# Moving second-product copies and squares from VectorE to ScalarE in the first groups of an MLP, and shifting a list of conditioning sums by a step

## The chip, the cores and the metric

The kernel runs on one core of one Trainium2 chip. The metric is the device time of one execution in microseconds (us); lower is better. The engines carry the profile's names: PE is TensorE's matmuls and PEld its weight loads, DVE is VectorE, ACT is ScalarE, POOL is GpSimd, and SP is SyncE, which issues the DMAs.

## The reference, cut to what matters

The program is a two-layer diffusion backbone over 512 latent tokens and 256 context tokens of width 1024. Each layer is a token mixer (pooling in layer 0, attention in layer 1) and then an MLP with 4096 inner units:

```python
def sq_relu_mlp(h, w_in, w_out):
    return jnp.square(jax.nn.relu(h @ w_in)) @ w_out
...
        m_lat = sq_relu_mlp(modulate(rms_norm(x, g_mlp_pre[i]), sh2, sc2), w_mlp_in[i], w_mlp_out[i])
        x = x + gt2 * rms_norm(m_lat, g_mlp_post[i])
```

The shift, scale and gate vectors come from the conditioning vectors `c` (latent tokens) and `c_ctx` (context tokens):

```python
def ada_mods(cond, w, b):
    m = (jax.nn.silu(cond) @ w + b)[..., None, :]
    return jnp.split(m, N_MOD, axis=-1)
```

All values are fp32.

## The kernel before

**Arithmetic.** A matrix product in fp32 accuracy is made of three products of rounded operands: each operand is split into a high part (a copy in the rounded type, usually on ACT) and a low part (operand minus high part, on DVE), and PE adds high x high, high x low and low x high.

**The first MLP (`mlp0`).** The 768 tokens are six row tiles of 128. The 4096 inner units are 16 groups of 256. For each group there is a first product (tokens by `w_mlp_in`), then ReLU and square, then a second product (squares by `w_mlp_out`), which is added up over the groups in the array `acc`. Group 0 and group 1 make the first product in the ordinary way (class `Inner`, line 553 for the matmuls). Later groups use a scheme with seven block products instead of eight (class `Seven`, line 672); it needs sums of blocks of the tokens, made once in `sums` (lines 617 to 620), and sums of blocks of the weights, made for each group in `weights_sums` (lines 638 to 655).

**Squares.** `Inner.square` takes the ReLU of a half group (`r`), squares it on ACT straight into the high part (line 572), squares it again on DVE into a tile `q` (line 573), and subtracts (line 574). `Seven.run` does it in another way: it squares in place on ACT (698), copies to the high part on ACT (699) and subtracts on DVE (700).

**The second product.** `out_mm` makes it for one row tile: two banks of 512 columns and twelve matmuls (line 768). There are four such banks in all (pool `psB`), which other small products share. `out_ev` takes the banks to `acc`. For group 0 it copies (line 776), for later groups it adds (line 780). Two of the six tiles, 1 and 4, are "seeded" in later groups: ACT copies the running sum from `acc` into the banks first (line 760), PE adds onto it, and ACT copies the result back (line 778). The seeding of a tile is left out while a counter `stale` is above zero; `ada_fin` sets it to 4, and each `out_mm` lowers it by 2. The weights of the second product are split into one slot (lines 126 and 129), which is free again when the matmuls of the group before are done.

**Conditioning sums.** A part of the shift, scale and gate vectors is computed beside the MLP on DVE: `ada_sum` loads 1 MB of `w_ada` and multiplies it by the conditioning vector, one instruction for each of eight blocks and each condition (lines 263 and 268), then transposes and reduces (271, 272). A list `work` holds 24 such sums, alternating between one for two conditions and one for a single condition. `ada_step` takes the next from the list. It is called at the start of a group (`extra0`, from group 1 on) and in the middle of `Seven.run` (`mid0`, groups 1 to 13), 27 times in all. Three calls after the fourth sum of a vector, `ada_fin` closes the vector: eight small matmuls (line 280) and an addition. Loads go through three staging buffers (`raw`), shared by the weights of the MLP and `w_ada`.

**Spilled rows.** Before the MLP the residual rows `xr` (six tiles) are written to memory (`spill_rows`, line 594), since `sums` reuses their place; `before0` closes that place again and loads the rows back ahead of the last stage, `finish`. The tiles' rows are made in the order 4, 5, 0, 1, 2, 3.

**Order.** The compiler plans the order on each engine: each engine executes its own instructions strictly in that order and waits where an operand or a place isn't ready. Instructions given to `keep_in_program_order` keep their place; in the first stage this holds for the loads that SP issues.

Of the kernel before, what the change touches and what calls it, by code (L numbers as in the profile page):

```python
# [12 lines left out]
AF = mybir.ActivationFunctionType  # L13
ALU = mybir.AluOpType
# [8 lines left out]
TOK = LAT + CTX  # L23
NL = LAT // P
NT = TOK // P
# [28 lines left out]
def backbone(ctx: ExitStack, tc, x, c, ctx_in, c_ctx, w_ada, b_ada, g_mix_pre, g_mix_post,  # L54
# [3 lines left out]
    sy, ve, sc, gp, te = nc.sync, nc.vector, nc.scalar, nc.gpsimd, nc.tensor  # L58
# [9 lines left out]
    def residents(stack):  # L68
        pool = stack.enter_context(tc.tile_pool(name="residents", bufs=1, side="right"))
        return (pool.tile([P, NT, D], F32, name="xr"), pool.tile([P, 2, D], F32, name="gate"),  # L70
                pool.tile([P, D], BF16, name="junk"))
# [40 lines left out]
    def work_tile():  # L112
        return tmp.tile([P, D], F32, tag="t", name="work")

    def sm_tile(tag):
        return small.tile([P, 8], F32, tag=tag, name=tag, bufs=2 if tag == "gc" else 8)
# [124 lines left out]
    def ada_out(i, m, j, ps, nc_, w=2):  # L241
        at = m * KT + 2 * j
        ve.tensor_tensor(out=mods[i][:, at:at + w, 0:nc_], in0=ps.rearrange("p (b c) -> p b c", c=nc_),
                         in1=cols[:, i * 48 + at: i * 48 + at + w].unsqueeze(2).broadcast_to([P, w, nc_]),
                         op=ALU.add)
        if (i, m) == (0, SH1):
            ve.tensor_scalar(out=minus[:, 2 * j:2 * j + w], in0=mods[i][:, at:at + w, 0:nc_], scalar1=-1.0,
                             scalar2=None, op0=ALU.mult)
        if m in (SC1, SC2):
            s = 0 if m == SC1 else 1  # L250
            g0 = 96 + s * 16 + i * KT + 2 * j
            ve.scalar_tensor_tensor(out=avec[i][s][:, 2 * j:2 * j + w, 0:nc_], in0=mods[i][:, at:at + w, 0:nc_],
                                    scalar=1.0,
                                    in1=cols[:, g0:g0 + w].unsqueeze(2).broadcast_to([P, w, nc_]),
                                    op0=ALU.add, op1=ALU.mult)
# [19 lines left out]
    def ada_fin(i, m, parts, nc_):  # L275
        n = 4 * nc_
        ps = psB.tile([P, 512], F32, tag="b", name="psada")
        stale[0] = 4
        for a in range(4):
            te.matmul(ps[32 * a:32 * a + 32, 0:2 * n], sel,  # L280
                      parts.rearrange("p (u c b a) -> p a u b c", c=nc_, b=2, a=4)[:, a], start=True, stop=True)
        ada_out(i, m, 0, ps[:, 0:2 * n], nc_, 8)
# [23 lines left out]
    def gate_diag(i, m, ci, to=None):  # L306
        to = ci if to is None else to
        gc = gate_cols(i, m, ci)
        gh = small.tile([P, 2, KT], F32R, tag="gh", name="gh", bufs=2)
        ve.tensor_copy(gh[:, 0, :], gc)  # L310
        ve.tensor_tensor(out=gh[:, 1, :], in0=gc, in1=gh[:, 0, :], op=ALU.subtract)
        dg = [tmp.tile([P, KT, P], F32R, tag="t", name="diag") for _ in range(2)]
        for z, d in enumerate(dg):
            ve.tensor_tensor(out=d, in0=ident.unsqueeze(1).broadcast_to([P, KT, P]),
                             in1=gh[:, z, :].unsqueeze(2).broadcast_to([P, KT, P]), op=ALU.mult)
        for h in range(2):
            ps = psB.tile([P, 512], F32, tag="b", name="psg")
            for z, d in enumerate(dg):
                te.matmul(ps, onesr[:, 0:1].broadcast_to([P, P]), d[:, 4 * h:4 * h + 4, :], start=(z == 0), stop=(z == 1))
            sc.copy(gate[:, to, 512 * h:512 * h + 512], ps)  # L320
# [210 lines left out]
    class Inner:  # L531
# [36 lines left out]
        def square(self, f):  # L568
            hi, lo = self.hid
            r = self.relu(f)  # L570
            q = work_tile()[:, 0:self.ntok]
            sc.activation(hi[:, f, :], r, AF.Square)
            ve.tensor_tensor(out=q, in0=r, in1=r, op=ALU.mult)
            ve.tensor_tensor(out=lo[:, f, :], in0=q, in1=hi[:, f, :], op=ALU.subtract)
# [15 lines left out]
    S = {}  # L590

    def spill_rows():
        for t in (4, 5, 0, 1, 2, 3):
            tc.keep_in_program_order(sy.dma_start(spill[:, t], xr[:, t]))

    def sums():
# [175 lines left out]
    def out_ev(i, parts, t, cols=HALVES):  # L772
        for (c0, w), ps in zip(cols, pso[t]):
            d = accv[:, t, c0:c0 + w]
            if parts[0][0] == 0:
                ve.tensor_copy(d, ps)
            elif seeded[t]:
                sc.copy(d, ps)
            else:
                ve.tensor_tensor(out=d, in0=d, in1=ps[:, 0:w], op=ALU.add)  # L780

    def finish(i, parts, order, last, also=()):
        st = Steps()
        for z in also:
            st.at(*z)
        for n, t in enumerate(order):
            cols = THIRDS if (i, t) == (1, NL - 1) else HALVES
            st.at(5.2 * n, out_mm, i, parts, t, cols)
            st.at(5.2 * n + 5.2, out_ev, i, parts, t, cols)
            last(st, n, t)  # L790
        st.run()

    def mlp0(inner, hids, order, extra, mid, last, before_last):
        aH, aL = inner.a
        one = lambda z: Ring([z], True)
        wi = w_in(0, 1, one(unit[1]), True)
        spill_rows()
        for f in range(2):
            inner.square(f)
        wo_ = w_out(0, 0, one(unit[2]))  # L800
        sums()
        for g in range(NG - 1):
            if g:
                wo_, products = w_out(0, g, one(unit[2])), weights_sums(g + 1)
            part = (g, inner.hid, wo_)
            extra(g)
            if g:
                inner = Seven(products, hids[(g + 1) % len(hids)])
            else:
                inner = Inner(g + 1, wi, aH, aL, hids[(g + 1) % len(hids)], chunks0, TOK)  # L810
            inner.run((lambda: mid(g)) if g < NG - 2 else None)
            if g == NG - 2:
                wo_ = w_out(0, NG - 1, one(unit[1]))
            else:
                for t in range(NT):
                    out_mm(0, [part], t)
                    out_ev(0, [part], t)
        before_last()
        finish(0, [part, (NG - 1, inner.hid, wo_)], order, last)
# [128 lines left out]
    work, due = [], []  # L948
# [4 lines left out]
    def ada_step():  # L953
        for u in [u for u in due if u[0] <= 0]:
            ada_fin(*u[1:])
        due[:] = [(u[0] - 1, *u[1:]) for u in due if u[0] > 0]
        if work:
            i, m, nc_, j, at = work.pop(0)
            ada_sum(i, m, j, nc_, parts[0][:, at + 8 * nc_ * j:at + 8 * nc_ * j + 8 * nc_])
            if j == 3:  # L960
                due.append((2, i, m, parts[0][:, at:at + 32 * nc_], nc_))
# [5 lines left out]
    def head_gains():  # L967
        sy.dma_start(grow[:, 0, :], g_q[0].partition_broadcast(P))
        sy.dma_start(grow[:, 1, :], g_k[0].partition_broadcast(P))
        ve.tensor_scalar(out=grow[:, 0, :], in0=grow[:, 0, :], scalar1=float(HD) ** -0.5, scalar2=None, op0=ALU.mult)  # L970

    def extra0(g):
        if g == 1:
            pinned[0] = False
        if g == 4:
            head_gains()
        if g:
            ada_step()
        if g == 2:
            sc.activation(sm_tile("sm")[:, 7:8], nhalf[:, 0:1], AF.Exp)  # L980
# [68 lines left out]
    def w_chunk(ch, kk, wait=None, pin=False):  # L1049
        chunks.setdefault(ch, []).append(  # L1050
            qring[0].load(w_qkv[0, 512 * kk:512 * kk + 512, 512 * ch:512 * ch + 512]
                      .rearrange("(k p) n -> p k n", p=P), 512, pin, wait))
# [90 lines left out]
    def before0():  # L1143
        nonlocal xr, gate, junk
        S["held"].close()
        xr, gate, junk = residents(held[1])
        gate_diag(0, GT2, 0)
        gate_diag(0, GT2, 1)
        for t in (4, 5, 0, 1, 2, 3):
            sy.dma_start(xr[:, t], spill[:, t])  # L1150
        qring.append(Ring([unit[0], unit[2], unit[1]]))
        w_chunk(2, 0, raw0)
# [169 lines left out]
    def last1(st, n, t):  # L1322
# [3 lines left out]
        st.at(5.2 * n + 7.8, fin_b, t)  # L1326

    mlp0(first[0], hids0, (4, 5, 0, 1, 2, 3), extra0, mid0, last0, before0)
    mlp1(first1[0], last1)

# [53 lines left out]
```

## Time and profile before

| | us |
|---|---|
| median of 3 runs | 1190.38 (1189.02 to 1190.64) |
| the profiled execution's own time | 1189.55 |
| its span, first to last instruction | 1187.8 |
| PE busy in the span | 1147.0 |
| DVE busy | 950.5 |
| ACT busy | 624.1 |

The profile is one execution. A span is the time from its first to its last instruction; the execution's own time is 1.75 us longer. "Busy" is the time in which an engine had an instruction in work, and an engine may be busy and still not be what sets the end. A row of the order of time gives start, duration, engine, line, operation, output and inputs; in brackets stand the idle time ahead of it and the instruction that ended it. "Granted clock" is the share of its full clock at which PE was let run.

### The profile page before, as it was taken

The numbers are of one execution on the slowest core, as the hardware profiler recorded it, in microseconds if no ns is written. First come the engines' busy times: TensorE is split into PE (matmuls) and PEld (weight loads), VectorE is DVE, ScalarE is ACT, GpSimd is POOL, SyncE is SP. The second block draws the span as 40 slices with busy tenths as digits, with TensorE's granted clock in tenths as the row PEclk, the third lists the DMA queues.
The fourth block names the chain that finished last, engine by engine and source line by source line (L and its number), as shares of the span: only waits on it lengthen the run. The fifth ranks groups of instructions, "written<-read, shape, count | busy, mean of one in ns | idle before, by whom it ended". The sixth has DMA issues, their size and how long they took to land.

```text
span 1187.8 us, 15989 instructions
## 1 busy us (share of the span) xinstructions
PE 1147.0 (97%) x6170; PEld 990.3 (83%) x6170; DVE 950.5 (80%) x1564; ACT 624.1 (53%) x1063; POOL 67.7 (6%) x120
## 2 busy tenths in 40 slices
PE   5899999999999999999999999999899999999997
PEld 3679789989899889988887889998888888888886
DVE  3787968889889888986587689978687788778876
ACT  4666435443445444544576378872676346435522
POOL 2030000000000000000142210001100000000001
PEclk9899999999999999999999999999999999999999
DMA  9984134443444443333431301105344133314312
GB/s 338 363 292 178 36 107 142 142 142 107 144 136 146 142 142 95 130 131 107 179 105 36 107 1 36 37 4 195 122 141 154 46 120 133 113 39 142 107 33 109
DMA packets 100011, 147.84 MB, mean 124 GB/s; under 512 B 2736, under 2 KB 75872, under 8 KB 99936
## 3 DMA queue, kind: packets, MB, share of 16 engines
q1 hardware_dynamic: 99936, 146.84, 36.6%
q8 instruction: 48, 0.79, 0.3%
q14 instruction: 27, 0.22, 0.1%
HBM read 139.49 MB, written 7.34 MB: 124 GB/s over the span
## 4 chain that ended last, share of the span: by engine, by line
PE 47%; issue 33%; DVE 9%; ACT 5%; POOL 3%; DMA 2%; SPq 0%; POOLq 0%; DVEq 0%; ACTq 0%
PE pso L768 19%; PE psin L672 17%; PE po L1226 2%; PE psq L1015 2%; PE pss L1187 2%; POOL rs L169 1%; DVE rows L268 1%; PE psin L553 1%; DMA raw<-in_w_mlp_in 1%; POOL rs L1024 1%; ACT junk L154 1%; DVE sm L1191 1%; PE psada L225 1%; PE pspt L1212 1%; DVE units L129 1%
## 5 line engine op out<-in xcount | busy, mean ns | idle before, releaser
L768 PE MATMUL pso<-units,rb 128*128 128x512 f32 x1152 | 279.7, 394 | 4.0 <-ACT pso L760 2.9
L768 PEld LDWEIGHTS pso<-units,rb 128*128 128x128 f32 x1152 | 215.7, 189 | 47.9 <-ACT pso L760 3.6
L268 DVE SCALAR_TENSOR_TENSOR rows<-raw,cond,rows 128x256 f32<-128x256 f32 x280 | 122.0, 477 | 0.7
L780 DVE TENSOR_TENSOR acc<-acc,pso 128x512 f32<-128x512 f32 x135 | 88.5, 676 | 31.6 <-PE pso L768 31.3
L553 PE MATMUL psin<-ra,rb 128*128 128x512 f32 (+1 forms) x432 | 104.8, 342 | 2.4 <-ACT ra L363 1.6
L872 PE MATMUL pso<-units,pairs 128*128 128x512 f32 x336 | 82.3, 389 | 0.0
L553 PEld LDWEIGHTS psin<-ra,rb 128*128 128x128 f32 x432 | 70.3, 189 | 13.6 <-ACT ra L363 1.9
L553 PE MATMUL psin<-ra 128*128 128x512 f32 x256 | 80.6, 389 | 0.0
L872 PEld LDWEIGHTS pso<-units,pairs 128*128 128x128 f32 x336 | 63.1, 188 | 13.1
L876 DVE TENSOR_TENSOR acc<-acc,pso 128x512 f32<-128x512 f32 x72 | 48.6, 681 | 27.6 <-PE pso L872 27.6
L167 POOL TENSOR_SCALAR ms<-ss 128x1 f32<-128x1 f32 x20 | 11.4, 572 | 1010.5 <-ACT junk L154 998.8
L672 PE MATMUL psin<-ra,units 128*128 128x384 f32 x336 | 66.0, 338 | 0.7 <-ACT psin L684 0.6
L672 PE MATMUL psin<-sums,units 128*128 128x384 f32 x336 | 63.7, 337 | 0.3 <-ACT units L638 0.2
L672 PEld LDWEIGHTS psin<-ra,units 128*128 128x128 f32 x336 | 59.3, 188 | 4.2 <-ACT psin L684 0.9
L129 DVE TENSOR_TENSOR units<-raw,units 128x1024 fp32r<-128x1024 f32 (+2 forms) x49 | 55.2, 1151 | 7.3 <-ACT units L126 7.1
L672 PEld LDWEIGHTS psin<-sums,units 128*128 128x128 f32 x336 | 58.8, 188 | 2.4 <-ACT psin L680 0.7
L760 ACT COPY pso<-acc 128x512 f32<-128x512 f32 x42 | 24.3, 589 | 67.2 <-DVE acc L780 65.2
L553 PEld LDWEIGHTS psin<-ra 128*128 128x128 f32 x256 | 48.0, 188 | 10.0
L126 ACT CAST units<-raw 128x1024 fp32r<-128x1024 f32 (+2 forms) x49 | 47.2, 995 | 14.3 <-PE pso L768 10.3
L553 PE MATMUL psin<-rb 128*128 128x512 f32 (+1 forms) x144 | 52.7, 367 | 0.2 <-DVE rb L364 0.2
L1015 PE MATMUL psq<-units,ra 128*128 128x512 f32 x216 | 51.7, 392 | 0.0
L553 PE MATMUL psin<-rb,ra 128*128 128x512 f32 x128 | 49.8, 389 | 0.0
(253 smaller groups left out, 2350.2 us busy)
## 6 DMA issues: line engine op xcount, KB each, us to landing
raw<-in_w_ada SPq DMA_DIRECT2D x48, 1024.0 KB, 5.4
raw<-in_w_mlp_in SPq DMA_DIRECT2D x32, 1024.0 KB, 5.4
raw<-in_w_mlp_out SPq DMA_DIRECT2D x32, 1024.0 KB, 5.1
raw<-in_w_qkv SPq DMA_DIRECT2D x6, 1024.0 KB, 5.3
spill<-xr SPq DMA_DIRECT2D x10, 512.0 KB, 9.3
xr<-spill SPq DMA_DIRECT2D x10, 512.0 KB, 5.9
raw<-in_w_o SPq DMA_DIRECT2D x4, 1024.0 KB, 5.4
xr<-in_x SPq DMA_DIRECT2D x4, 512.0 KB, 4.4
```

Of the source, the lines that this page charges most:

```text
L126: a = sc.copy(hi, raw)
L129: b = ve.tensor_tensor(out=lo, in0=raw, in1=hi, op=ALU.subtract)
L268: ve.scalar_tensor_tensor(out=r, in0=raw[:, k, :], scalar=cond[:, k, c:c + 1], in1=r, op0=ALU.mult, op1=ALU.add)
L553: te.matmul(ps[:, bank, o:o + ln], w[:, k, fs], rhs, start=start, stop=(k == KT - 1 and n == 2), skip_group_check=len(ks) < KT)
L672: te.matmul(bank, w[k], a[k], start=start and k == 0 and m == 0, stop=stop and k == 3 and m == 2, skip_group_check=True)
L760: sc.copy(ps, accv[:, t, c0:c0 + w])
L768: te.matmul(pss[h][:, 0:cols[h][1]], a[:, f, ts_], w[:, f, cols[h][0]:sum(cols[h])], start=(n == 0 and not seeded[t]), stop=(n == len(seq) ...
L780: ve.tensor_tensor(out=d, in0=d, in1=ps[:, 0:w], op=ALU.add)
L872: te.matmul(ps, a, w, start=(m == 0), stop=(m == len(seq) - 1))
L876: ve.tensor_tensor(out=M[n][:, t], in0=M[n][:, t], in1=ps, op=ALU.add)
L1015: te.matmul(ps, a[:, k, sl], w[:, k % 4, :], start=(k == 0 and n == 0), stop=(k == KT - 1 and n == 2))
L1187: te.matmul(ps[:, c2, 0:384], a[:, sl], b[:, kv, 384 * c2:384 * c2 + 384], start=(n == 0), stop=(n == 2))
```

## The change

It has five parts, all around the first MLP. (1) `Inner.square` for 768 tokens, which is groups 0 and 1, works as `Seven.run` does: it squares in place on ACT, copies to the high part on ACT, subtracts on DVE, and no tile `q` is needed. (2) In group 0's second product, 8 of the 12 copies from the banks to `acc` go from DVE to ACT; DVE keeps the right halves of tiles 1, 2, 4 and 5. (3) `extra0` no longer calls `ada_step` in group 1, so there are 26 calls, and every sum of the list is done one call later than before. (4) The last vector to be closed, whose time would be after the last call, is closed in `before0`. (5) The rows are spilled in the order 0 to 5.

```diff
         def square(self, f):
             hi, lo = self.hid
             r = self.relu(f)
+            if self.ntok == TOK:
+                sc.activation(r, r, AF.Square)
+                sc.copy(hi[:, f, :], r)
+                ve.tensor_tensor(out=lo[:, f, :], in0=r, in1=hi[:, f, :], op=ALU.subtract)
+                return
             q = work_tile()[:, 0:self.ntok]
...
     def spill_rows():
-        for t in (4, 5, 0, 1, 2, 3):
+        for t in range(NT):
             tc.keep_in_program_order(sy.dma_start(spill[:, t], xr[:, t]))
...
             if parts[0][0] == 0:
-                ve.tensor_copy(d, ps)
+                (ve.tensor_copy if c0 and t % 3 else sc.copy)(d, ps)
...
         if g == 4:
             head_gains()
-        if g:
+        if g > 1:
             ada_step()
...
     def before0():
         nonlocal xr, gate, junk
         S["held"].close()
+        assert not work
+        for u in due:
+            ada_fin(*u[1:])
         xr, gate, junk = residents(held[1])
```

## The prediction

> **What bounds the kernel now.** I read the page's busy shares first, then the table of stretches stage by stage, then PE in order of time where a stretch shows idle PE, and then who was late there. Part 1 of the page:
>
> ```profile
> PE 1147.0 (97%) x6170; PEld 990.3 (83%) x6170; DVE 950.5 (80%) x1564; ACT 624.1 (53%) x1063; POOL 67.7 (6%) x120
> ```
>
> PE sets the end, so a change can win only where PE idles or runs slower. This one works on the first MLP. Its stretches (length; busy time of PE, PEld, DVE, ACT, POOL with counts; granted clock; share and GB/s of DMA):
>
> ```profile
> 105.00:157.00 52.00, 48.37 (x245) 42.63 (x244) 50.85 (x80) 24.33 (x32) 0.00 (x0) 0.97 0.20 65
> 188.20:500.00 311.80, 310.71 (x1571) 277.67 (x1570) 279.06 (x529) 147.42 (x220) 0.00 (x0) 1.00 0.41 134
> ```
>
> The second row is the steady loop, ten groups of 31 us: PE is full but for 311.80 - 310.71 = 1.09 us, and DVE works some 28 us a group. The first row, in which the first groups start up, is the other way round: DVE is busy 50.85 of 52 us, PE lacks 3.63, ACT works less than half the time, and the clock is under 1. PE there, in order of time:
>
> ```profile
> 133.85 11.08 PE L768 MATMUL pso<-units,rb 128*128 128x512 f32 x48
> 145.38 0.73 PE L768 MATMUL pso<-units,rb 128*128 128x512 f32 x2 [0.46 <-ACT units L126]
> 148.09 0.50 PE L768 MATMUL pso<-units,rb 128*128 128x512 f32 x1 [1.97 <-ACT pso L760]
> 149.48 5.12 PE L768 MATMUL pso<-units,rb 128*128 128x512 f32 x13 [0.89 <-ACT pso L760]
> ```
>
> And the stretch right behind:
>
> ```profile
> 150.00:154.00 4.00, 4.00 (x11) 3.13 (x12) 4.00 (x6) 1.95 (x2) 0.00 (x0) 0.57 0.25 77
> ```
>
> Group 0's second product ends at 144.9 us; then PE waits 0.46 + 1.97 + 0.89 = 3.32 us. Behind that the clock falls: 4.00 us at 0.57 are 4.00 x 0.43 = 1.72 us of lost PE work. Together 5.04 us. Who caused the two longer waits:
>
> ```profile
> 147.45 0.59 ACT L760 COPY pso<-acc 128x512 f32<-128x512 f32 x1 [1.17 <-DVE acc L776]
> 148.12 0.68 DVE L776 COPY acc<-pso 128x512 f32<-128x512 f32 x1
> 148.84 0.59 ACT L760 COPY pso<-acc 128x512 f32<-128x512 f32 x1 [0.80 <-DVE acc L776]
> ```
>
> There are four banks for these products and a row tile takes two. Group 1's seeded tile needs the two of group 0's last tile, which PE had filled by 144.9, but whose copies stood in DVE's queue; the last began at 148.12, 3.2 us late. The chain of waits over 105 to 160 us names DVE lines for most of what isn't PE's own work:
>
> ```profile
> by line: PE pso L768 12.7%; DVE work L617 12.3%; DVE acc L776 12.3%; DMA raw<-in_w_mlp_in 9.2%; DVE rows L268 8.3%; issue 7.4%; PE psin L672 6.7%; DVE sums L620 6.4%; DVE units L129 6.4%; DVE rb L620 3.4%; DVE rb L574 3.3%; DVE work L573 3.
> ```
>
> **The change part by part.** Prices come from the groups of 105 to 157 us (count | busy us, mean ns | idle before):
>
> ```profile
> L776 DVE COPY acc<-pso 128x512 f32<-128x512 f32 x12 | 7.9, 681 | 0.0
> L268 DVE SCALAR_TENSOR_TENSOR rows<-raw,cond,rows 128x256 f32<-128x256 f32 x14 | 6.2, 475 | 0.0
> L573 DVE TENSOR_TENSOR work<-work 128x768 f32<-128x768 f32 x4 | 3.8, 952 | 1.0 <-ACT work L560 1.0
> L572 ACT ACTIVATE rb<-work 128x768 fp32r<-128x768 f32 x4 | 3.4, 848 | 0.1
> L619 ACT CAST sums<-work 128x768 fp32r<-128x768 f32 x6 | 5.0, 832 | 3.5 <-DVE work L617 2.0 <-DMA raw<-in_w_mlp_in 1.4
> L271 DVE STREAM_TRANSPOSE raw<-rows 128x256 f32<-128x256 f32 x2 | 0.8, 416 | 0.0
> L272 DVE TENSOR_REDUCE parts<-raw 128x16 f32<-128x512 f32 x1 | 0.7, 672 | 0.0
> L263 DVE TENSOR_SCALAR rows<-raw,cond 128x256 f32<-128x256 f32 x2 | 0.6, 349 | 0.0
> ```
>
> ACT makes the same copy out of these banks elsewhere (min/median/max ns):
>
> ```profile
> L778 ACT COPY acc<-pso x42: 564/588/593, 157.0 to 558.0; 128x512 f32<-128x512 f32 x42
> ```
>
> *Copies.* DVE keeps the right halves of tiles 1, 2, 4 and 5. Eight move: DVE -8 x 0.681 = 5.4 us, ACT +8 x 0.588 = 4.7 us. The last tile's two halves are then copied on two engines side by side.
>
> *Squares.* Four times, DVE loses L573 (3.8 us in all); ACT squares in place, as long as L572, and adds a copy like L619: 4 x 0.832 = 3.3 us. The high part comes some 0.84 us later. What hides that is the distance to its reader:
>
> ```profile
> 109.40 0.85 ACT L572 ACTIVATE rb<-work 128x768 fp32r<-128x768 f32 x1
> 126.26 5.64 PE L768 MATMUL pso<-units,rb 128*128 128x512 f32 x24
> 145.26 0.95 DVE L574 TENSOR_TENSOR rb<-work,rb 128x768 fp32r<-128x768 f32 x1
> ```
>
> Group 0's squares of 109.4 are first multiplied at 126.3. Group 1's low part ended at 146.2, out of DVE's backlog, and comes earlier without it.
>
> *First conditioning sum.* 6.2 + 0.8 + 0.7 + 0.6 = 8.3 us leave DVE in this stretch. They are moved, not saved: the list still has 24 sums, and the last one falls into group 13's start instead of group 12's middle.
>
> Sum for the stretch: DVE 50.85 - 5.4 - 3.8 - 8.3 = 33.4 of 52, ACT 24.33 + 4.7 + 3.3 = 32.3. Neither is the bound then; PE is. DVE's lateness of 3.2 us stands against 17.5 us taken off its queue, so I count the two longer waits as gone.
>
> What is late next is the split of group 1's output weights, since its slot is free only when PE is through with group 0's:
>
> ```profile
> 144.29 1.99 ACT L126 CAST units<-raw 128x1024 fp32r<-128x1024 f32 x2 [5.60 <-PE pso L768]
> ```
>
> With ACT's half copy (1.0 us) and DVE's subtraction (1.2 us, half of the 2.35 in the steady loop's row below) the first low half is there at 146.5. If PE has nothing else from 145.4 on, it waits 1.1 us; if group 2's products are ready, because the weight sums come earlier, it waits 0. Ends 0 and 1.1; I take 0.5, since ACT, now with 32 us, may hold one copy back. Whether such a rest would still pull the clock down, these rows tell:
>
> ```profile
> 851.11 1.53 PE L349 MATMUL psx<-ident,acc 128*128 128x128 f32 x12 [1.60 <-DVE acc L514]
> 854.28 0.50 PE L553 MATMUL psin<-ra,rb 128*128 128x256 f32 x2 [1.64 <-ACT ra L363]
> ```
>
> ```profile
> 800.00:900.00 100.00, 96.54 (x508) 82.87 (x508) 75.06 (x106) 55.74 (x87) 8.74 (x17) 1.00 0.46 154
> ```
>
> Waits of 1.60 and 1.64 us close together left the clock at 1.00, so 1.1 us should too. The Trainium skill ("TensorE: Matmul & The Clock Gate", section Why this matters for your kernels) asks only that PE-idle gaps stay under about 3 us. By that rule alone three gaps of at most 1.97 us would not explain the fall at 150 us, its 1.72 us need not go with them, and the gain would be 1.72 us less. The trace bears this out at 851 us and speaks against it at 145 us.
>
> *The list moved by a step.* Sums for two conditions and for one alternate. So far the former ran at a group's start and the latter in its middle; now it is the reverse, and the middle is where DVE is dense:
>
> ```profile
> 203.11 0.48 DVE L268 SCALAR_TENSOR_TENSOR rows<-raw,cond,rows 128x256 f32<-128x256 f32 x1
> 213.90 2.35 DVE L129 TENSOR_TENSOR units<-raw,units 128x1024 fp32r<-128x1024 f32 x2
> 217.79 5.19 PE L768 MATMUL pso<-units,rb 128*128 128x512 f32 x22
> 222.82 2.27 PE L672 MATMUL psin<-ra,units 128*128 128x384 f32 x12
> ```
>
> Beginning with the one at 203.11, five single L268 stand ahead of the weight split at 213.90. Doubled, each adds 0.4 us or so (back to back nine take 3.64, next fence), and the opening multiply 0.26: 2.3 us. The first half of the split ends near 215.1 and is needed at 217.79: slack 2.7 us. It holds by 0.4 us, and PE could bring the product of 222.82 forward (2.27 us). I take 0. The ends are one irregular group, which is there already:
>
> ```profile
> 412.43 3.64 DVE L268 SCALAR_TENSOR_TENSOR rows<-raw,cond,rows 128x256 f32<-128x256 f32 x9
> 432.78 0.73 PE L768 MATMUL pso<-units,rb 128*128 128x512 f32 x2 [0.68 <-ACT units L126]
> 433.73 0.62 PE L672 MATMUL psin<-sums,units 128*128 128x384 f32 x2 [0.21 <-ACT units L638]
> ```
>
> It paid 0.68 + 0.21 = 0.89 us after sums had run as a block. Ends: -0.9 if it becomes regular, +10.7 if all twelve groups become like it.
>
> *Closing steps.* Each finished vector closes half a group later, the last one just ahead of the last stage; instructions are the same. Two groups instead of five lose the seed of tile 1, so six adds on DVE become six seeds and six copies on ACT; in the steady loop ACT has 147 of 312 us. 0, with cover on both engines.
>
> *Spill order.* SP issues the same six transfers, but tiles 4 and 5 behind tile 3, whose rows are written last; the output weights queued behind them start about two issues, 0.8 us, later.
>
> ```profile
> DMA to landing us min/median/max: 8.7/10.0/12.1
> 86.14 1.62 SPq L107 DMA_DIRECT2D raw<-in_w_mlp_out  x2
> 113.26 0.84 ACT L619 CAST sums<-work 128x768 fp32r<-128x768 f32 x1 [1.38 <-DMA raw<-in_w_mlp_in]
> ```
>
> Issued by 87, the spills land by 99; what overwrites the rows starts at 113.26. 0. The dropped sum's load isn't dropped: the next sum's block takes its place and holds its staging buffer longer, which leaves two for weights; the steady loop lives with that.
>
> Sum against the profiled execution's 1189.55 us: -3.32 - 1.72 + 0.5 = -4.5, so 1185.0. The median of the runs, 1190.38, lies 0.83 above that execution: 1185.9.
>
> **The rivals.**
>
> *Slower: the reversed sums hold up every group.* If the two-condition sum runs ahead of the weight split as a block, each of twelve groups pays 0.89 us: 1185.9 + 10.7 = 1196.6. It ends slower by over 0.2% from (4.5 + 2.4) / 12 = 0.58 us a group. For it: DVE's 28 of 31 us and a slack of only 0.4. Against: PE lost 1.09 us in ten groups in all.
>
> *No change: the stall stays in another form.* If group 1's product again stands directly behind group 0's in PE's fixed order and the longest gap and the slow clock stay, 0.46 + 0.89 = 1.35 us go: 1189.0. For it: the order is planned beforehand, not chosen by readiness. Against: the late engine loses a third of its work.
>
> *ACT becomes the bound.* If in each of six tiles one copy holds PE for its 0.588 us, 3.5 us come back: 1189.4. For it: eight of twelve copies in one queue with squares and splits. Against: 32 of 52 us.
>
> **How the numbers follow.** Forecast 0.62, stall stays 0.15, ACT 0.08, sums 0.15. About 0.2%, 2.4 us, is what a measurement of this kernel tells from no change. Of the sums' 0.15, 0.03 cost so little that it is still faster, 0.03 end within, 0.09 beyond; of the others' 0.23, 0.02 go beyond. Faster 0.65, same 0.24, slower 0.11. The forecast's own range is 1184.4 (no rest at 145 us, a regular loop) to 1187.4 (1.1 us of rest, one more irregular group). To hold 8 in 10 it takes in both rivals near 1189 and a little beyond: 1183.8 to 1190.5.
>
> **What would show it.** Right: near 145 us no PE gap over 1.1 us, a clock of 1.00 from 145 to 160, DVE under 40 of the 52 us, 48 seeds of L760's kind. Wrong: the gap moved behind an ACT copy or the split, with the clock still falling; or more than 2 us of idle PE in the steady loop, with the weight split last in the wait.

## Result and the profile after

The changed kernel takes 1179.72 us (median of 4 runs, 1179.53 to 1181.20) against 1190.19 us before (4 runs on the same chip, 1189.02 to 1190.64). The ratio is 0.9916, with a 95% interval of 0.9899 to 0.9933. The forecast was 1185.9 with a range of 1183.8 to 1190.5: the direction came out, the size was more than twice the one forecast, and the time lies 4 us below the range. The profiled execution after took 1179.53 us, its span is 1177.7 us, 10.1 us shorter than before. Two executions of the experiments below ran disturbed, at 1911.59 us (the profiled one of copies_squares) and 4029.18 us (one of skip_not_reversed); no figure below uses them.

Part 1 of the page, after:

```profile
PE 1142.0 (97%) x6170; PEld 988.8 (84%) x6170; DVE 941.6 (80%) x1546; ACT 638.0 (54%) x1087; POOL 67.4 (6%) x120
```

The three stretches of the prediction, after (columns as there):

```profile
105.00:157.00 52.00, 52.00 (x281) 48.10 (x282) 37.33 (x52) 32.33 (x48) 0.00 (x0) 1.00 0.25 82
150.00:154.00 4.00, 4.00 (x19) 3.33 (x19) 1.03 (x2) 0.12 (x1) 0.00 (x0) 1.00 0.81 261
188.20:500.00 311.80, 311.80 (x1586) 280.61 (x1585) 278.63 (x521) 154.61 (x230) 0.00 (x0) 1.00 0.40 132
```

In the first stretch PE now has no idle time and runs at full clock; DVE fell from 50.85 to 37.33 us. The third row deserves a second look. PE's busy time went up by 1.09 us only, but in the same 311.8 us it now does 1586 matmuls instead of 1571. Fifteen matmuls at some 0.2 us are 3 us: more than the 1.09 us of idle time that the row of before shows.

PE in order of time where the gaps were (the helper's five new lines move L768 to L773, L672 to L677, L760 to L765, L776 to L781, L778 to L783 and L780 to L785):

```profile
134.59 5.64 PE L773 MATMUL pso<-units,rb 128*128 128x512 f32 x24
140.07 0.87 PE L677 MATMUL psin<-sums,units 128*128 128x384 f32 x4
140.78 1.55 PE L773 MATMUL pso<-units,rb 128*128 128x512 f32 x6
142.17 1.20 PE L677 MATMUL psin<-sums,units 128*128 128x384 f32 x6
143.21 2.92 PE L773 MATMUL pso<-units,rb 128*128 128x512 f32 x12
145.97 2.61 PE L677 MATMUL psin<-sums,units 128*128 128x384 f32 x14
148.42 5.42 PE L773 MATMUL pso<-units,rb 128*128 128x512 f32 x23
```

No row has a bracket. Before, the second products of groups 0 and 1 stood back to back; now PE has first products of group 2 (L677) to put between them at 140.07, 142.17 and 145.97, because the weight sums that these need are no longer late on DVE: the last of their low halves is written there at 138.0 us, where before it was at 154.2. ACT and DVE beside it:

```profile
145.94 0.59 ACT L781 COPY acc<-pso 128x512 f32<-128x512 f32 x1
147.38 0.59 ACT L765 COPY pso<-acc 128x512 f32<-128x512 f32 x1
...
142.37 0.69 DVE L781 COPY acc<-pso 128x512 f32<-128x512 f32 x1 [2.35 <-PE pso L773]
145.88 1.23 DVE L129 TENSOR_TENSOR units<-raw,units 128x1024 fp32r<-128x1024 f32 x1 [2.82 <-ACT units L126]
147.02 0.69 DVE L781 COPY acc<-pso 128x512 f32<-128x512 f32 x1
```

DVE, which before had a backlog of 3.2 us here, waits 2.35 and 2.82 us for work. The rows of group 0's copies, the seeds and the copies back, by line:

```profile
L765 ACT COPY pso<-acc 128x512 f32<-128x512 f32 x48 | 27.9, 585 | 8.2 <-DVE acc L785 8.1
L783 ACT COPY acc<-pso 128x512 f32<-128x512 f32 x48 | 27.1, 586 | 43.6 <-PE pso L773 42.9
L781 ACT COPY acc<-pso 128x512 f32<-128x512 f32 x8 | 4.5, 587 | 2.9 <-PE pso L773 2.8
```

Eight copies at 587 ns (588 was forecast), and 48 seeds.

**Where the 10.1 us are.** PE does the same matmuls in nearly the same order, so I numbered them in both traces and compared the start of the one with the same number. Before minus after: 0.6 us at matmul 900 (126.7 us), all of it there by matmul 300, in the first 50 us, before the change can act (this figure varies between -0.7 and +1.4 over the kernels below, which begin alike; the reason is open); 6.5 us at matmul 1200 (194 us), so 5.9 from the group start-up; 9.9 us at matmul 3100 (570 us), so 3.4 from the steady loop; and 10.0 at the end. The first of the two gains was forecast as 4.5, the second as 0. "First gain" and "loop gain" below are these two differences against the trace of before, from matmul 900 to 1200 and from 1200 to 3100.

### The profile page after: what moved, and what is told of

Its sections match the earlier page's. It is cut to its first block, busy times and chain, and to the rows that moved or that the text cites. A ratio compares the mean times of both kernels' runs of the same rounds, so it can differ in the third digit from the quotient of the medians.

```text
span 1177.7 us, 15984 instructions
## 1 busy us (share of the span) xinstructions
PE 1142.0 (97%) x6170; PEld 988.8 (84%) x6170; DVE 941.6 (80%) x1546; ACT 638.0 (54%) x1087; POOL 67.4 (6%) x120
## 4 chain that ended last, share of the span: by engine, by line
PE 52%; issue 33%; DVE 6%; ACT 4%; POOL 3%; DMA 2%; SPq 0%; POOLq 0%; DVEq 0%; ACTq 0%
PE pso L773 22%; PE psin L677 18%; PE psin L553 3%; PE po L1234 2%; PE psq L1020 2%; PE pss L1195 2%; POOL rs L169 1%; PE psada L225 1%; PE psm L420 1%; POOL rs L1029 1%; ACT junk L154 1%; DVE sm L1199 1%; PE pspt L1220 1%; DVE rows L268 1%; DVE units L1223 1%
## 5 line engine op out<-in xcount | busy, mean ns | idle before, releaser
L773 PE MATMUL pso<-units,rb 128*128 128x512 f32 x1152 | 278.9, 392 | 0.0
L773 PEld LDWEIGHTS pso<-units,rb 128*128 128x128 f32 x1152 | 214.7, 188 | 41.1
L268 DVE SCALAR_TENSOR_TENSOR rows<-raw,cond,rows 128x256 f32<-128x256 f32 x280 | 127.3, 480 | 2.0
L785 DVE TENSOR_TENSOR acc<-acc,pso 128x512 f32<-128x512 f32 x129 | 85.4, 677 | 39.4 <-PE pso L773 39.3
L881 DVE TENSOR_TENSOR acc<-acc,pso 128x512 f32<-128x512 f32 x72 | 48.7, 683 | 26.4 <-PE pso L877 26.4
L677 PE MATMUL psin<-ra,units 128*128 128x384 f32 x336 | 65.5, 337 | 0.4 <-ACT psin L689 0.4
L677 PE MATMUL psin<-sums,units 128*128 128x384 f32 x336 | 64.0, 336 | 0.0
L677 PEld LDWEIGHTS psin<-ra,units 128*128 128x128 f32 x336 | 59.8, 188 | 3.9 <-ACT psin L689 0.5
L677 PEld LDWEIGHTS psin<-sums,units 128*128 128x128 f32 x336 | 58.9, 188 | 1.6
L783 ACT COPY acc<-pso 128x512 f32<-128x512 f32 x48 | 27.1, 586 | 43.6 <-PE pso L773 42.9
```

Of the source, the lines that this page charges most:

```text
L268: ve.scalar_tensor_tensor(out=r, in0=raw[:, k, :], scalar=cond[:, k, c:c + 1], in1=r, op0=ALU.mult, op1=ALU.add)
L677: te.matmul(bank, w[k], a[k], start=start and k == 0 and m == 0, stop=stop and k == 3 and m == 2, skip_group_check=True)
L773: te.matmul(pss[h][:, 0:cols[h][1]], a[:, f, ts_], w[:, f, cols[h][0]:sum(cols[h])], start=(n == 0 and not seeded[t]), stop=(n == len(seq) ...
L881: ve.tensor_tensor(out=M[n][:, t], in0=M[n][:, t], in1=ps, op=ALU.add)
```

## The experiments

Each run is compared with runs of the kernel before on the same chip, whose medians were 1190.4, 1191.01, 1190.59 and 1190.05 in the four groups of runs.

### Each part of the change alone

*copies*: part 2 alone.

```diff
-                ve.tensor_copy(d, ps)
+                (ve.tensor_copy if c0 and t % 3 else sc.copy)(d, ps)
```

> Only part 2: eight of group 0's twelve copies go to ACT. Theory A (backlog): PE's gap near 145 us exists because DVE's queue runs 3.2 us late, and whatever takes more than that off the queue removes it with its slow clock; 5.4 us leave here, so the gap goes and about 5.9 us of the 10.1 (1184 to 1185 us), while the irregular group near 432 us stays. Theory B (order): PE's order still puts group 1's matmuls directly behind group 0's, so the rest of 1.1 us or more stays; 4 us (1186). Theory C: the copies hardly matter, the dropped sum does; 1 us or less.

*squares*: part 1 alone, the six lines added to `square`.

> Only part 1: the squares of groups 0 and 1 on ACT, 3.8 us off DVE, of which half stands before 126 us and half before the last copies. Theory A (backlog): more than the 3.2 us of lateness, so the gap shrinks to at most 1.1 us and the clock stays up; 4 to 6 us (1184 to 1186 us). Theory B (the last tile's copies need ACT): the last two copies still stand in DVE's queue behind other work; the gap keeps more than 1.5 us, 1 to 2 us gained (1188 to 1189).

*shift*: parts 3 and 4 alone.

```diff
-        if g:
+        if g > 1:
             ada_step()
...
         S["held"].close()
+        assert not work
+        for u in due:
+            ada_fin(*u[1:])
```

> Parts 3 and 4 alone: first sum left out of group 1, list a step later, last vector closed ahead of the last stage; copies and squares as before. Theory A (backlog): 8.3 us leave DVE before the gap, the gap goes (5.9 us), and the irregular group at 432 us becomes regular (2.3 us): 1181.5 to 1182.5 us, most of the whole. Theory B: the copies on DVE keep part of the gap, 4 us gained in all (1186). If the irregular group has nothing to do with the list, it stays and the gain is 5.9 at most (1184.3).

*skip_not_reversed*: shift, with a list that begins with a sum for one condition. In every group the kinds of sums then stand as before the change.

```diff
-        work.append((*dual[n // 4], n % 4, 64 * (n // 4 % 2)))
         work.append((*lone[n // 4], n % 4, 128 + 32 * (n // 4 % 2)))
+        work.append((*dual[n // 4], n % 4, 64 * (n // 4 % 2)))
```

> Parts 3 and 4, but the list begins with the one-condition sums, so that after the skip the one-condition sums run in a group's middle and the two-condition sums at its start, as before the change. Against the run with the list merely shifted it tells whether the reversal matters in the steady loop. Theory A: the reversal is what made the group at 432 us regular; here it stays irregular or another one appears: about 2 us slower than the shifted list (1183.5 to 1184.5 us). Theory B: the time of the closings alone did it; same as the shifted list (within 0.7 us).

| | us (range, runs) | ratio (95%) | first gain | loop gain |
|---|---|---|---|---|
| copies | 1186.69 (1185.63 to 1188.28, 7) | 0.9970 (0.9959 to 0.9980) | 3.6 | -0.6 |
| squares | 1187.13 (1185.84 to 1188.24, 9) | 0.9973 (0.9964 to 0.9983) | 3.8 | -0.9 |
| shift | 1181.81 (1181.18 to 1182.88, 4) | 0.9928 (0.9912 to 0.9945) | 5.0 | 3.3 |
| skip_not_reversed | 1181.72 (1181.47 to 1183.05, 3) | 0.9932 (0.9916 to 0.9949) | 5.0 | 2.7 |

The stretch from 144 to 152 us of copies, squares and shift, in this order:

```profile
144.00:152.00 8.00, 6.82 (x28) 5.24 (x29) 7.57 (x11) 3.83 (x5) 0.00 (x0) 1.00 0.59 207
...
144.00:152.00 8.00, 6.38 (x28) 4.64 (x27) 8.00 (x13) 4.79 (x6) 0.00 (x0) 1.00 0.54 176
...
144.00:152.00 8.00, 7.30 (x38) 6.33 (x38) 6.21 (x7) 4.89 (x7) 0.00 (x0) 1.00 0.61 187
```

And PE's waits in it, in copies (three rows), squares (two) and shift (one):

```profile
144.00 0.73 PE L768 MATMUL pso<-units,rb 128*128 128x512 f32 x2 [0.46 <-ACT units L126]
145.43 0.50 PE L768 MATMUL pso<-units,rb 128*128 128x512 f32 x1 [0.71 <-ACT pso L760]
146.41 0.98 PE L672 MATMUL psin<-sums,units 128*128 128x384 f32 x4 [0.47 <-ACT units L638]
...
144.96 0.73 PE L773 MATMUL pso<-units,rb 128*128 128x512 f32 x2 [0.46 <-ACT units L126]
146.85 0.97 PE L677 MATMUL psin<-sums,units 128*128 128x384 f32 x4 [1.16 <-ACT units L643]
...
147.00 0.50 PE L768 MATMUL pso<-units,rb 128*128 128x512 f32 x1 [0.70 <-ACT pso L760]
```

Taking 5.4, 3.8 or 8.3 us off DVE's queue each leaves some 0.7 to 1.6 us of the 3.32 us of labelled waits, and in this stretch of the three profiles the clock did not fall. The gains do not add: 3.6 + 3.8 + 5.0 = 12.4 against the 5.9 of the whole. A shared backlog gives that; a fixed price for each copy or square would not. The loop gain comes with the shift alone, and stays when the sums are not reversed.

### Two parts together

*copies_squares*: parts 1 and 2. *copies_squares_2* is the same kernel once more.

> Parts 1 and 2 together, list and closings as before. Theory A (backlog): 9.2 us off DVE, nearly three times the lateness; the planned order now has 24 matmuls of group 2's products between group 0's and group 1's second products; the first stage loses nothing (5.9 us against before), and the steady loop keeps its 2 to 3 us: 1184 to 1185. Theory C (each part alone gives 3.6 to 3.8, so together 7.4): 1183. If the dropped sum is needed to close the gap: 4 us, 1186.5.

> Parts 1 and 2 again, since the first profile was disturbed; its undisturbed runs gained 5.0 us. Theory A: the first stage 5.9 us as in the changed kernel, so no gap at 145 us; the loop keeps its 432 us gap (loss about 0.9 us more there, as the groups start earlier). If the first stage shows less than 5, the dropped sum is needed there as well.

*copies_shift*: the changed kernel without part 1 and with the old spill order. *squares_shift*: the same without part 2 instead. *all_old_spill*: all parts but the spill order.

> The changed kernel without part 1: squares stay on DVE. Theory A: with the list shifted 0.87 us of gap were left, put down to ACT's seeds waiting for banks that DVE empties; the copies on ACT take that away, so 5.9 us in the first stage and 3.3 in the loop, the same as the changed kernel within 0.7 us (1179.5 to 1181). If the squares matter by themselves: 1 us or more slower.

> The changed kernel without part 2: copies stay on DVE. Theory A (backlog): 12.1 us off DVE, the 0.87 us that the shifted list alone leaves go as well; first stage 5.9, loop 3.3: within 0.7 us of the changed kernel. Theory B (the last tile's copies need ACT): 0.9 us remain, 1181 to 1182.

> The changed kernel with the old order of spills. PE, DVE, ACT and POOL have the same instructions in the same order. Theory: nothing hangs on it, 1179.7 within 0.7 us, and the first 50 us vary by themselves. Rival: the spills landed late for something; 0.6 us or more slower.

| | us (range, runs) | ratio (95%) | first gain | loop gain |
|---|---|---|---|---|
| copies_squares | 1185.57 (1185.19 to 1187.08, 5) | 0.9957 (0.9941 to 0.9974) | | |
| copies_squares_2 | 1184.89 (1184.23 to 1186.26, 4) | 0.9959 (0.9944 to 0.9973) | 6.5 | -0.9 |
| copies_shift | 1181.07 (1180.74 to 1181.41, 4) | 0.9916 (0.9899 to 0.9934) | 6.4 | 2.7 |
| squares_shift | 1180.57 (1180.03 to 1181.19, 4) | 0.9921 (0.9906 to 0.9936) | 6.4 | 2.7 |
| all_old_spill | 1179.84 (1179.56 to 1181.82, 4) | 0.9918 (0.9903 to 0.9933) | 5.9 | 3.4 |

The stretch from 144 to 152 us, copies_squares_2 and squares_shift:

```profile
144.00:152.00 8.00, 8.00 (x46) 7.72 (x45) 5.76 (x9) 4.04 (x7) 0.00 (x0) 1.00 0.51 166
...
144.00:152.00 8.00, 8.00 (x41) 7.20 (x40) 3.42 (x4) 3.88 (x6) 0.00 (x0) 1.00 0.43 137
```

Any two parts close the start-up gap wholly; the third adds nothing there. (Their first gains of 6.4 to 6.5 lie above the whole change's 5.9, and with the shift the loop gain is lower by as much: the border between the two columns is soft by some 0.6 us.) Given the shift, the squares or the copies could each be left out, and the time is within 1.4 us of the whole change. The spill order is worth nothing that can be measured.

### Where the loop gain comes from

The shift does two things in the loop: the sums change places, and the closings (`ada_fin`) come later, so that two groups instead of five lose the seed of tile 1. Seven kernels take these apart.

*reversed_only*: before, with the two lines of the list swapped and nothing left out.

> The kernel before, but the list begins with the one-condition sum; nothing is skipped. In group 1 about 4 us of DVE work move behind the gap, and in the steady loop the two-condition sums run in the middle. Theory A (backlog): the first gap shrinks to 1.5 to 2.2 us and the clock stays up, 3.6 to 4 us; the steady loop keeps its irregular group, as the closings stay (1186.5 to 1187). Theory B (the reversal regularises the loop): 2.3 us more (1184.3). If the reversal harms the loop, as my rival had it: 1195 or more.

*closings_late*: before, with the closings one call later and the last in `before0`.

```diff
-                due.append((2, i, m, parts[0][:, at:at + 32 * nc_], nc_))
+                due.append((3, i, m, parts[0][:, at:at + 32 * nc_], nc_))
```

> The kernel before with one edit: finished vectors close one call later (and the last one ahead of the last stage), at the places that they have after the change; sums, copies and squares as before. Theory A (the closings and the seeds they suspend made the group at 432 us irregular): the first stage keeps its gap and slow clock, the steady loop gains 2.7 to 3.3 us: 1187 to 1187.7. Theory B (the shift of the sums did it): no change, 1190.

*seeds_kept*: before, with every seed of tile 1 kept. It leaves out the pause in the seeding that a closing asks for, so its output isn't the reference's and only its time is of use.

```diff
-        stale[0] = 4
+        stale[0] = 0
```

> The kernel before, but a closing no longer suspends seeding, so tile 1 is seeded in 13 groups instead of 8; closings stay where they are. Theory A1 (the lost seeds, two more adds on DVE and another order of the banks, cause the loss at 432 us): the steady loop gains 2 to 3.3 us (1187 to 1188). Theory A2 (the two closings of neighbouring half groups themselves cost it): the gap at 432 us stays, 1189.5 to 1190.5.

*lost_seeds* and *lost_apart*: the changed kernel, with three more groups that lose the seed of tile 1; in the first they lie next to a closing, in the second apart from one.

```diff
             head_gains()
+        if g in (5, 9, 13):          # lost_apart: (4, 8, 12)
+            stale[0] = 4
```

> The changed kernel, but seeding is suspended in three more groups (5, 9 and 13), so that tile 1 loses its seed in five groups as before the change. Theory A1 (lost seeds): 2 to 3.3 us slower than the changed kernel, with a gap behind one of these groups: 1182 to 1183. Theory A2 or B (closings or sums): 1179.7, within 0.7 us.

> The changed kernel, but seeding is suspended in groups 4, 8 and 12 as well, two groups away from those in which closings suspend it (6 and 10). Five lost seeds as before the change, but no longer in neighbouring groups. Theory A1 (any lost seed costs): 3 to 3.5 us slower in the loop than the changed kernel, as when groups 5, 9 and 13 lose it. Theory A5 (only next to the groups where closings let two sums overlap): within 0.7 us in the loop.

*seed_tile2* (on the changed kernel) and *before_seed_tile2* (on before): a group that loses tile 1's seed seeds tile 2 instead, so that DVE has no more adds than in other groups.

```diff
-t in (1, 4) and stale[0] <= 0
+(t in (1, 4) or t == 2 and not seeded[1]) and stale[0] <= 0
```

> The changed kernel, and where a closing takes the seed of tile 1, tile 2 is seeded in its place, so that all thirteen groups have two seeded tiles. Theory A1 (each lost seed costs about 1 us of the loop): two groups get theirs back, 1 to 2 us faster than the changed kernel: 1178 to 1179. Theory A3 (only the case with five lost seeds was beyond what the loop can take): 1179.7, within 0.7 us.

> The kernel before with the same edit: closings where they are, but the five lost seeds go to tile 2. Theory A1 (lost seeds, two adds of 0.68 us on DVE each): the steady loop gains 2.5 to 3.3 us as with the seeds simply kept (1187 to 1188), first gap unchanged. Theory A4 (it is the seed of tile 1 that orders the banks well, not the work on DVE): under 1 us, 1190.

| | us (range, runs) | ratio (95%) | first gain | loop gain |
|---|---|---|---|---|
| reversed_only | 1189.11 (1187.12 to 1189.90, 10) | 0.9980 (0.9970 to 0.9989) | 2.1 | -3.0 |
| closings_late | 1189.94 (1187.78 to 1191.28, 10) | 0.9991 (0.9982 to 1.0001) | -0.7 | 0.7 |
| seeds_kept | 1186.85 (1185.92 to 1187.85, 5) | 0.9967 (0.9953 to 0.9981) | -0.1 | 3.1 |
| lost_seeds | 1186.12 (1185.22 to 1187.70, 4) | 0.9961 (0.9946 to 0.9977) | 5.9 | -0.2 |
| lost_apart | 1182.12 (1181.70 to 1182.45, 4) | 0.9933 (0.9916 to 0.9949) | 5.9 | 2.3 |
| seed_tile2 | 1181.51 (1181.25 to 1182.68, 4) | 0.9922 (0.9904 to 0.9940) | 5.9 | 2.6 |
| before_seed_tile2 | 1189.53 (1185.91 to 1190.93, 10) | 0.9990 (0.9979 to 1.0001) | -0.3 | 1.1 |

The loop's row in reversed_only, closings_late, seeds_kept, lost_seeds and lost_apart, in this order (before has x1571, after x1586):

```profile
188.20:500.00 311.80, 308.06 (x1556) 274.55 (x1555) 275.93 (x520) 149.03 (x221) 0.00 (x0) 1.00 0.39 129
...
188.20:500.00 311.80, 310.67 (x1570) 277.80 (x1569) 275.12 (x521) 151.37 (x227) 0.00 (x0) 1.00 0.40 131
...
188.20:500.00 311.80, 311.80 (x1586) 280.98 (x1585) 277.60 (x525) 157.74 (x239) 0.00 (x0) 1.00 0.41 134
...
188.20:500.00 311.80, 309.80 (x1567) 277.19 (x1567) 279.34 (x522) 150.10 (x221) 0.00 (x0) 1.00 0.39 130
...
188.20:500.00 311.80, 311.65 (x1577) 279.05 (x1576) 279.02 (x520) 149.80 (x219) 0.00 (x0) 1.00 0.40 132
```

PE's waits from 157 to 557 us, after and then lost_seeds (us in total, times, longest; the one of after stands at 556.88 us, at the loop's end, and lost_seeds has it too, with 0.61 us at 560.74, just outside this stretch):

```profile
PE psin L677 <- ACT psin L689: 0.4, 1, 0.4
...
PE pso L773 <- ACT pso L765: 0.9, 1, 0.9
PE psin L677 <- DVE units L644: 0.6, 1, 0.6
PE pso L773 <- DVE units L129: 0.4, 1, 0.4
```

reversed_only is worth a second look in the start-up too. PE there, and its stretch from 144 to 152 us:

```profile
144.31 0.73 PE L768 MATMUL pso<-units,rb 128*128 128x512 f32 x2 [0.46 <-ACT units L126]
145.74 0.49 PE L768 MATMUL pso<-units,rb 128*128 128x512 f32 x1 [0.70 <-ACT pso L760]
146.72 1.58 PE L672 MATMUL psin<-sums,units 128*128 128x384 f32 x4 [0.48 <-ACT units L638]
...
144.00:152.00 8.00, 6.51 (x20) 5.01 (x21) 8.00 (x12) 4.20 (x6) 0.00 (x0) 0.79 0.32 99
```

These are the waits of copies to a hundredth or two, and yet the clock fell here, 8 x 0.21 = 1.7 us of it in this stretch, and not in copies. The first gains differ by as much: 2.1 against 3.6.

Shown for the loop: keeping the seeds gives before nearly the whole loop gain (3.1 of 3.4), and taking three away from the changed kernel takes it back (3.36 + 0.18 = 3.5). It depends on where they are lost: away from the closings, three lost seeds cost 1.1 us. Reversing the sums is no gain: by itself it costs 3.0 us, and in the changed kernel, with fewer lost seeds, it costs nothing. Nor is that a fixed price of reversed sums with five lost seeds: lost_seeds has both, its seeds lost in other groups, and stands only 0.2 us behind before.

Two of my ideas fell. Moving the closings alone should have brought the loop gain if the lost seeds were all; it brought 0.7. And if the price were DVE's two extra adds in such a group, seeding tile 2 instead should have paid it back; on before it brought 1.1 of 3.1, and on the changed kernel nothing (1181.51 against 1179.72). By exclusion that leaves tile 1's own seed, together with what else stands near the closing in the planned order; no run shows it directly. Why it is tile 1, I have not settled: the planner gives each of these kernels another order, and the traces show late operands in another place each time.

## Why the prediction was right or wrong

**Right, the mechanism of the start-up.** The prediction said that DVE's late copies hold the banks that group 1's seeds need, and that the slow clock goes with the gap. Each part of the change alone shortened the gap by half or more, and any two ended it. The clock stayed at 1.00 in every kernel without the gap and fell in all four that keep it at full length (before, closings_late, seeds_kept, before_seed_tile2); with half of it, it could go either way (copies against reversed_only). DVE at 37.33 us is under the 40 that it named; it is above 33.4 since the stretch now holds 281 matmuls instead of 245 and the work that goes with them. The 48 seeds and the clock of 1.00 came out as told, and so did the spill order at 0. That ACT's 32.33 us meet the 32.3 so closely is luck in part: the forecast's sum counts 32 + 8 + 4 = 44 instructions of ACT in this stretch, and 48 ran.

**Wrong, the size of the gap (term 3.32, and 0.5 of rest).** The terms 3.32 + 1.72 - 0.5 = 4.5 measured 5.9. The rest was 0, because group 2's products were ready in time; of the two ends that the prediction named, 0 was right. The other 0.9 us were in the rows already: a bracket counts idle time from the modelled end of the matmul before it, so it hides a part of what PE loses. Counted from start to start, the row of 48 matmuls gives (11.08 - 0.39) / 47 = 0.227 us a matmul, where 0.39 is the time that the profile gives the last one. Of the same kind there are 48 + 2 + 1 + 13 = 64 between 133.85 and the next product, whose row in before is

```profile
154.44 0.87 PE L672 MATMUL psin<-sums,units 128*128 128x384 f32 x4
```

That is 20.59 us for 64 x 0.227 = 14.55 us of work: 6.0 us lost, where the brackets and the clock made 5.04.

**Wrong, the list and the closings (terms 0 and 0).** Together they measured 3.4 us of gain. The lower end of the list's term, 0.9 us for the one irregular group becoming regular, was the right event with too low a price. Around the two rows at 432.78 and 433.73 that the prediction quoted, PE in order of time before the change reads

```profile
431.48 0.62 PE L672 MATMUL psin<-ra,units 128*128 128x384 f32 x2
...
434.39 2.00 PE L672 MATMUL psin<-ra,units 128*128 128x384 f32 x10
436.23 0.63 PE L768 MATMUL pso<-units,rb 128*128 128x512 f32 x2
436.94 0.62 PE L672 MATMUL psin<-sums,units 128*128 128x384 f32 x2
437.40 2.89 PE L768 MATMUL pso<-units,rb 128*128 128x512 f32 x12
```

From 431.48 to 437.40, 5.92 us, PE began 16 narrow matmuls ((2.27 - 0.33) / 11 = 0.176 us each, from a row of 12) and 4 wide ones: 16 x 0.176 + 4 x 0.227 = 3.7 us. It lost 2.2, not 0.89. Counted in the same way over 157 to 575 us, the changed kernel loses 3.3 us less than before; what is not in this group is scattered in pieces of 0.1 to 0.2 us, most of them without a bracket. The other step that failed is "Closing steps ... 0, with cover on both engines": it counted instructions and asked which engine had room, while the runs show that the loop's time depends on the lost seeds (3.1 us on before, 3.5 on the changed kernel). The later closings alone are not the whole of it: with them, and two groups instead of five that lose the seed, closings_late gained 0.7. The other 2.7 came only with the sums moved as well, and why stays open.

**The rest, 0.6 us,** was gained in the first 50 us, ahead of the change. It lies within the spread named above; the medians, 10.5 us apart, say the same as the spans within it.

**The rivals.** The reversed sums do hold up groups in one kernel where five groups lose the seed: 3.0 us in reversed_only, not 10.7, and with the seeds lost in other groups (lost_seeds) 0.2. In the changed kernel no labelled wait in the loop is for the weight split; the order there is another one, so the 0.4 us of slack can't be put to the test. The stall in another form, behind one ACT seed of 0.70 us, is what shift alone shows; copies or squares on top remove it. ACT was never the bound.

**The Trainium skill's rule on gaps.** The prediction weighed the Trainium skill ("TensorE: Matmul & The Clock Gate", section Why this matters for your kernels), which asks that PE-idle gaps stay under about 3 us. By it the 1.72 us of slow clock need not have gone with the gaps. The runs decide against the rule as a sufficient one: the clock fell with every gap of the full kind, whose longest wait was 1.97 to 2.31 us in the four kernels, and once with waits of at most 0.70 us (reversed_only). The prediction's own remark, that waits of 1.60 and 1.64 us close together left the clock alone, was no safe ground either, as the last section shows.

## What to carry to other kernels

Where one engine is full in a short start-up stretch and others are not, moving any work off its queue pays up to what its backlog costs the engine that sets the end (5.9 us here), and then nothing: find the backlog first, and move no more than that. Price a stall by the matmuls done in a stretch, or from start to start, since the brackets, even with the slow clock added, missed a sixth of the loss in the start-up, and nearly two thirds of it in the loop. In an order planned beforehand, an edit that moves work between groups can be worth more through what it does to a shared pool of banks than through the instructions it moves.

## What was not expected of the hardware

The fall of the clock depends on more than the length of one gap. Three gaps of at most 1.97 us within 4.6 us brought it down at 150 us before, and waits of 0.46, 0.70 and 0.48 us did so in one kernel and not in another. Waits of 1.6, 1.6 and 0.2 us ahead of the last stage's products, which are the same in all of these kernels, brought it down in 8 of the 17 profiles and left it alone in 9. Here in copies, where it fell, and after, where it did not (PE in order of time, then the stretch from 840 to 860 us, each):

```profile
846.81 1.53 PE L349 MATMUL psx<-ident,acc 128*128 128x128 f32 x12 [1.61 <-DVE acc L514]
849.98 0.50 PE L553 MATMUL psin<-ra,rb 128*128 128x256 f32 x2 [1.64 <-ACT ra L363]
...
840.00:860.00 20.00, 16.53 (x114) 15.45 (x114) 12.72 (x15) 11.50 (x20) 2.23 (x4) 0.91 0.22 75
...
841.21 1.53 PE L349 MATMUL psx<-ident,acc 128*128 128x128 f32 x12 [1.59 <-DVE acc L514]
844.38 0.50 PE L553 MATMUL psin<-ra,rb 128*128 128x256 f32 x2 [1.64 <-ACT ra L363]
...
840.00:860.00 20.00, 16.92 (x101) 14.90 (x102) 15.15 (x17) 14.14 (x19) 0.37 (x1) 1.00 0.19 59
```

20 x (1 - 0.91) = 1.8 us at most are at stake; matched matmul by matmul, the kernels in which it fell lost 1.3 to 1.5 us there. The traces show one thing more. In all 17 the granted clock is either full or half, and its changes lie at whole multiples of 3.413 us from one another. Cut along that grid, the last stage of squares, where the clock fell, and of closings_late, where it stayed full behind these two slots, reads

```profile
845.06:848.48 3.42, 1.81 (x16) 1.61 (x15) 0.75 (x1) 1.03 (x3) 0.79 (x2) 1.00 0.38 153
848.48:851.89 3.41, 1.55 (x11) 1.10 (x10) 2.92 (x6) 3.41 (x8) 0.00 (x0) 1.00 0.00 0
851.89:855.30 3.41, 3.41 (x17) 3.41 (x17) 2.55 (x4) 3.31 (x4) 0.00 (x0) 0.50 0.00 0
...
848.32:851.73 3.41, 1.82 (x17) 1.62 (x15) 1.09 (x2) 1.15 (x2) 0.79 (x2) 1.00 0.38 154
851.73:855.14 3.41, 1.78 (x14) 1.54 (x14) 2.25 (x5) 2.85 (x6) 0.00 (x0) 1.00 0.00 0
```

In this stage PE was busy for at most 3.48 us of two neighbouring slots wherever the clock fell behind them, and for at least 3.59 of any two where it did not. So it seems to be the place of the same waits on the grid that decides, and that place is luck. The split was found afterwards, and in the start-up it does not hold alone: there the clock also fell behind a single slot with 1.15 us of busy PE (closings_late) and one with 1.77 (reversed_only), with a full slot before it. No run here moves the waits along the grid.
